# Matrix product with batch normalization: the last pair of tile 4 and the last chunk of tile 5 go back into the common order

## The chip, the cores and the metric

The kernel runs on one core of a Trainium2 chip. The metric is the device time of one execution in microseconds, as a median of several runs. Beside it stands one profiled execution, whose span is the time from its first to its last recorded instruction.

## The reference

The input `x` has 16 x 512 rows of 1024 numbers (8192 rows in all), the weight is 1024 x 768. Each of the 768 output columns is normalized over all 8192 rows and then scaled and shifted:

```python
y = np.matmul(x, weight)
mean = np.mean(y, axis=(0, 1), keepdims=True)
var = np.var(y, axis=(0, 1), keepdims=True)
y_norm = (y - mean) / np.sqrt(var + eps)
return (gamma * y_norm + beta).astype(np.float32)
```

No column can be written before its product is there for all 8192 rows, since its mean and variance need all of them.

## The kernel before

The 8192 rows are cut into C = 16 chunks of 512, the 768 columns into NT = 6 tiles of 128. Rows of `x` are loaded by GpSimd's queue as bf16 and transposed by VectorE into `xT`, one buffer for a chunk, so that TensorE can contract over K = 1024 in eight matmuls of 128.

Tiles 0 to 2 (GA = 3) are finished first, while `x` still arrives; their output follows while TensorE works on the rest. Tiles 3 to 5 are computed with the columns on the partitions: `mm` (L190) makes `y_ps`, 128 columns x 512 rows in one PSUM bank, by eight matmuls (L194). Chunks 0 to 4 of these tiles are done during the load, chunks 5 to 15 afterwards, tile by tile (loop at L559).

For each chunk of a tile, `bn` (L301) has VectorE take the statistics of the bank (`bn_stats`, six numbers, into `stats`), and `keep` (L332) has ScalarE copy the bank as bf16 into `y_sb`. After the 16th chunk the statistics are aggregated (`bn_aggr`), and mean and variance become a scale and a shift for each column: `finish_var` and `finish_affine` (L338, L344) for tiles 3 and 4, `finish` (L351) for tile 5. Then, for each tile:

- `norm` (L365) scales and shifts `y_sb` in place, on VectorE or ScalarE;
- `turn_y` (L377) puts 128x128 transposes on a list. `mm` takes one from this list behind each of its matmuls (`turn_one`, L386), so that the transposes run among the matmuls of the tile that follows;
- `out_copy` (L390) issues what is left of the transposes of its group and copies the PSUM bank `o_ps` to SBUF as f32 on ScalarE. For tiles 3 and 4 a group is a pair of chunks (128x1024) and goes into a piece of `ring`, a buffer of 6144 words in which pieces follow one another around; for tile 5 a group is one chunk (128x512) and goes into an `xT` buffer, called `o_sb`;
- `store` (L405) issues the DMA to HBM on SyncE's queue: 512 KB for a pair, 256 KB for a chunk, in runs of 512 bytes.

The order on every engine is written out by hand. Each step is put in a list with a time, `at(t, step, ...)`, in planned microseconds; the list is sorted by time, and `seq` (L75) ties each instruction to the one before it on its engine. `pe` is the planned time of TensorE. So the times only decide the order; the chip runs it as fast as data and buffers allow. Eight PSUM banks and the buffers of `ring` and `xT` go around in that order too.

At the end of the kernel two things leave the common way:

- HELD = 1: of the eight pairs of tile 4, `outputs` (L527) leaves out the last one (chunks 14 and 15). `held_outputs` (L539) puts its norms three planned microseconds before the end of tile 5's matmuls, and its transposes, copy and store right behind that end.
- The last chunk of tile 5 is done in two halves of 256 rows, in a bank each: `mm_half`, `bn_half`, `keep_half` (L315, L326, L329). The statistics of the first 14 chunks are aggregated beforehand by `sum_up` (L308) into one entry of `fin`; chunk 14 and the two halves add an entry each, and the aggregate in `finish` is over `fin`, 21 numbers for each column, in place of `stats`, 96 numbers.

`last_outputs` (L548) then does the 16 chunks of tile 5: all norms on VectorE, all copies on ScalarE.

Of the kernel before, what the change touches and what calls it, by code (L numbers as in the profile page):

```python
# [10 lines left out]
def kernel(  # L11
# [23 lines left out]
    nc = tc.nc  # L35
    f32 = mybir.dt.float32
    bf16 = mybir.dt.bfloat16
    AF = mybir.ActivationFunctionType
    ALU = mybir.AluOpType
# [5 lines left out]
    P = 128  # L45
    NT = N // P
    KQ = K // 4
    CH = 512
    RT = CH // P
    C = M // CH  # L50
    QR = 256
    QPC = CH // QR
    JW = KQ // 64
# [4 lines left out]
    GA = 3  # L58
    COLS = (0, 5, 10, 15)
    NA = GA * P  # L60
    HELD = 1
    GY = 3

    x_flat = x.flatten_outer_dims()
# [2 lines left out]
    singles = ctx.enter_context(tc.tile_pool(name="singles", bufs=1))  # L67
# [3 lines left out]
    psum = ctx.enter_context(tc.tile_pool(name="psum", bufs=8, space=bass.MemoryType.PSUM))  # L71
# [3 lines left out]
    def seq(bi):  # L75

        ins = bi.ins
        prev = last.get(ins.engine)
        if prev is not None:
            tc.add_manual_dep(  # L80
                ins, prev,
                mybir.DependencyInfo(mybir.DependencyClass.NoSync, mybir.DependencyReason.DATA),
                reason="order",
            )
        last[ins.engine] = ins.name
        return bi
# [10 lines left out]
    w_sb = singles.tile([P, JW, 2, N], bf16)  # L97
# [13 lines left out]
    stats = singles.tile([P, NT, C, 6], f32)  # L111
    ngamma = singles.tile([P, NT], f32)
    nscale = singles.tile([P, 1], f32)
    fin = singles.tile([P, 21], f32)
    msq = singles.tile([P, GA], f32)
    mv = singles.tile([P, NT, 2], f32)
    std = singles.tile([P, NT], f32)
# [7 lines left out]
    xs, xT, py, ygrp, yrow, ops, ost, aff = {}, {}, {}, {}, {}, {}, {}, {}  # L125
# [168 lines left out]
    def y(nt, c):  # L294
        key, i = ((nt, c // GY), c % GY) if nt >= GA else ((0, c), nt)
        if key not in ygrp:
            y_sb = ypool.tile([P, GY, CH], bf16, tag="y")
            ygrp[key] = y_sb
        return ygrp[key][:, i]

    def bn(nt, c):  # L301
        if (nt, c) == (NT - 1, C - 2):
            seq(nc.vector.bn_stats(fin[:, 3:9], py[nt, c]))
            return
        i = c if nt >= GA else COLS.index(c)
        seq(nc.vector.bn_stats(stats[:, nt, i, :], py[nt, c]))  # L306

    def sum_up():  # L308

        seq(nc.vector.memset(fin[:, 0:1], float((C - 2) * CH)))  # L310
        seq(nc.vector.bn_aggr(fin[:, 1:3], stats[:, NT - 1, 0:C - 2, :]))
        seq(nc.vector.tensor_scalar(
            fin[:, 2:3], fin[:, 2:3], float((C - 2) * CH), None, op0=ALU.mult))

    def mm_half(q):  # L315
        y_ps = psum.tile([P, CH], f32, tag="b")
        py["half", q] = y_ps[:, 0:QR]
        for jw in range(JW):
            for e in range(2):
                seq(nc.tensor.matmul(  # L320
                    y_ps[:, 0:QR], w_sb[:, jw, e, (NT - 1) * P:NT * P],
                    xT[C - 1][:, jw, q * QR:(q + 1) * QR, e],
                    start=(jw == 0 and e == 0), stop=(jw == JW - 1 and e == 1),
                ))

    def bn_half(q):  # L326
        seq(nc.vector.bn_stats(fin[:, 9 + 6 * q:15 + 6 * q], py["half", q]))

    def keep_half(q):  # L329
        seq(nc.scalar.copy(y(NT - 1, C - 1)[:, q * QR:(q + 1) * QR], py.pop(("half", q))))  # L330

    def keep(nt, c):  # L332
        seq(nc.scalar.copy(y(nt, c), py.pop((nt, c))))  # L333
# [16 lines left out]

    def finish(nt):  # L351
        one = slice(nt, nt + 1)
        src = stats[:, nt, :, :] if nt < NT - 1 else fin
        seq(nc.vector.bn_aggr(mv[:, nt, :], src))
        seq(nc.scalar.activation(std[:, one], mv[:, nt, 1:2], AF.Sqrt, bias=eps_sb, scale=1.0))
        seq(nc.vector.scalar_tensor_tensor(
            tmp[:, one], mv[:, nt, 0:1], -1.0, gamma_sb[:, one], op0=ALU.mult, op1=ALU.mult,
        ))
        seq(nc.vector.reciprocal(rstd, std[:, one]))
        seq(nc.vector.tensor_mul(scale[:, one], rstd, gamma_sb[:, one]))  # L360
        seq(nc.vector.scalar_tensor_tensor(
            shift[:, one], tmp[:, one], rstd, beta_sb[:, one], op0=ALU.mult, op1=ALU.add,
        ))
# [51 lines left out]
    def at(t, fn, *args):  # L415
        events.append((t, len(events), fn, args))
# [31 lines left out]
    pe = 0.0  # L448
# [12 lines left out]
    def unit(nt, c, span, jws=range(JW)):  # L461
        nonlocal pe
        pe = max(pe, arrive[c * RT + RT - 1])
        at(pe, mm, nt, c, jws)
        pe += span
        if jws[-1] == JW - 1:
            at(pe + 0.2, bn, nt, c)
            at(pe + 1.0, keep, nt, c)
# [13 lines left out]
    pe = max(pe, arrive["w", 2])  # L482
# [44 lines left out]
    def outputs(nt, t0, step):  # L527
        for b in range(C // 2):
            tb = t0 + step * b
            if nt == NT - 2 and b >= C // 2 - HELD:  # L530
                held.append(b)
                continue
            for i in range(2):
                at(tb - 2.2 + 0.5 * i, norm, nt, 2 * b + i, "act" if tb < tr + 2.0 and i == 0 else "dve")
            at(tb, turn_y, (nt,), 2 * b * CH, 2 * RT)
            at(tb + 2.2, out_copy, (nt,), 2 * b * CH, "act")
            at(tb + 2.3, store, (nt,), 2 * b * CH, 2 * RT)

    def held_outputs(nt, t0):  # L539

        for i, b in enumerate(held):
            for j in range(2):
                at(t0 - 3.0 + 0.4 * (2 * i + j), norm, nt, 2 * b + j, "dve")
            at(t0 + 0.05, turn_y, (nt,), 2 * b * CH, 2 * RT)
            at(t0 + 0.7 + 0.1 * i, out_copy, (nt,), 2 * b * CH, "act")
            at(t0 + 0.75 + 0.1 * i, store, (nt,), 2 * b * CH, 2 * RT)

    def last_outputs(nt, t0):  # L548

        for c in range(C):  # L550
            tb = t0 + 0.6 * c
            at(tb - 1.2, norm, nt, c, "dve")
            at(tb, turn_y, (nt,), c * CH, RT)
            at(tb + 0.5, out_copy, (nt,), c * CH, "act", True)
            at(tb + 0.6, store, (nt,), c * CH, RT)

    held = []
    halves = [range(JW // 2), range(JW // 2, JW)]
    for nt in range(GA, NT):  # L559
        for c in range(EARLY, C):  # L560
            if (nt, c) == (NT - 1, C - 1):
                for q in range(QPC):
                    at(pe, mm_half, q)
                    pe += 0.9
                    at(pe + 0.2, bn_half, q)
                    at(pe + (0.4 if q == 0 else 1.0), keep_half, q)
                at(pe - 2.4, sum_up)
                continue
            for jws in halves:
                unit(nt, c, MM_US / 2 + (0.12 if nt == GA else 0.17), jws)  # L570
        if nt < NT - 1:
            at(pe + 0.55, finish_var, nt)
            at(pe + 1.6, finish_affine, nt)
        else:
            at(pe + 0.55, finish, nt)
        if nt == GA:
            outputs(nt, S + 41.0, 2.0)
        elif nt < NT - 1:
            outputs(nt, pe + 4.6, 1.85)
        else:  # L580
            held_outputs(nt - 1, pe)
            last_outputs(nt, pe + 3.0)

    events.sort(key=lambda e: e[:2])
# [37 lines left out]
```

## Time and profile before

| what | us |
|---|---|
| median of 3 runs | 220.02 |
| lowest, highest run | 219.51, 225.25 |
| the profiled execution's own time | 220.02 |
| its span | 218.2 |
| PE busy (share of the span) | 199.1 (91%) |
| VectorE (DVE) busy | 151.5 (69%) |
| GpSimd (POOL) busy | 134.4 (62%) |
| ScalarE (ACT) busy | 120.4 (55%) |
| bytes read from HBM, written | 36.71 MB, 25.17 MB |

The span is 1.8 us shorter than the execution's time; what lies around it is not on the page. PE is TensorE's matmul side, PEld its weight loads, SP is SyncE, and a q behind an engine's name (SPq) marks its issuing of DMAs. L194 is line 194 of the kernel above. Times in a timeline are microseconds from the start of the span; "x7" counts instructions; what stands in brackets is the idle time ahead of an instruction and what ended it. A matmul's record is longer than its share of TensorE, since matmuls are pipelined; the chain of waits gives each one the time by which it moves the next.

The planned order by the time in the profile: the loads and tiles 0 to 2 take up to about 126 us; tile 3's matmuls, tile 4's and tile 5's follow, with the output of tiles 0 to 2, 3 and 4 running beside them; the last matmul of tile 5 ends at 197.6, its first store is issued at 200.8 and its last at 213.4.

### The profile page before, as it was taken

Reading aid. Unit: us, or ns where it says so; the run is one execution under the profiler, and the core shown is the slowest. Engines: PE = TensorE matmul, PEld = TensorE weight load, DVE = VectorE, ACT = ScalarE, POOL = GpSimd, SP = SyncE. Lnnn points to the kernel's source line nnn. Section 1 sums busy time; section 2 is a strip of 40 time slices with the busy share of each in tenths; the row PEclk is TensorE's granted clock in tenths of the full one; section 3 lists DMA queues with packets and bytes.
Section 4 is the critical chain, followed back from the end, with each engine's and each line's share of the span. In section 5 each row is a group of like instructions: output and inputs, shape, how many; then the busy total and the mean of one; then the engine's idle time right before and its main releaser. Section 6 shows DMA issues by size and latency. Waiting matters only on the chain.

```text
span 218.2 us, 3442 instructions
## 1 busy us (share of the span) xinstructions
PE 199.1 (91%) x1162; PEld 105.2 (48%) x1178; DVE 151.5 (69%) x264; ACT 120.4 (55%) x226; POOL 134.4 (62%) x153
## 2 busy tenths in 40 slices
PE   7997999999999999999999999999999999996500
PEld 2462454545554566545566544444444556555300
DVE  3221968886988889998744459988899999358400
ACT  2000562644453466645666414867766899977910
POOL 8787777778685599962658403999999960000000
PEclk9999999999999999999999999999999999999965
DMA  5999999999999999994000000698789799999997
GB/s 64 161 180 178 192 196 195 197 196 196 196 190 194 197 196 196 196 196 67 0 5 0 0 0 0 241 376 312 286 300 366 256 343 342 347 347 323 306 288 199
DMA packets 70161, 43.75 MB, mean 200 GB/s; under 512 B 4096, under 2 KB 69632, under 8 KB 70144
## 3 DMA queue, kind: packets, MB, share of 16 engines
q0 software_dynamic: 34624, 18.36, 61.7%
q1 hardware_dynamic: 35520, 25.18, 36.1%
q8 instruction: 9, 0.15, 0.3%
q14 instruction: 8, 0.07, 0.1%
HBM read 36.71 MB, written 25.17 MB: 284 GB/s over the span
## 4 chain that ended last, share of the span: by engine, by line
PE 74%; DVE 6%; DMA 5%; ACT 4%; POOL 3%; issue 3%; DVEq 0%; POOLq 0%
PE y_ps L194 40%; PE y_ps L184 29%; ACT o_sb L401 3%; PE o_ps L388 3%; DMA w_sb<-in_weight_dram 3%; DVE y_sb L372 3%; DMA ring<-in_x_dram 3%; POOL w_sb L147 2%; DVE ring L278 1%; DVE stats L306 1%; POOL ring L160 1%; PE y_ps L320 1%; PE a_ps L270 1%; PE tot_ps L230 1%; ACT ring L401 0%
## 5 line engine op out<-in xcount | busy, mean ns | idle before, releaser
L194 PE MATMUL y_ps<-xT_sb,w_sb 128*128 128x512 bf16 (+1 forms) x469 | 115.3, 382 | 2.8 <-DMA w_sb<-in_weight_dram 1.5
L194 PEld LDWEIGHTS <-w_sb 128*128 128x128 bf16 x484 | 46.1, 96 | 60.6 <-issue 3.4
L333 ACT CAST y_sb<-y_ps 128x512 bf16<-128x512 f32 x59 | 34.7, 589 | 52.3 <-DVE stats L306 49.5
L184 PE MATMUL y_ps<-w_sb,xT_sb 128*128 128x384 bf16 x384 | 63.4, 326 | 0.0
L306 DVE BATCH_NORM_STATS2 stats<-y_ps 128x6 f32<-128x512 f32 x58 | 39.2, 685 | 21.7 <-PE y_ps L194 21.4
L160 POOL DMA_DIRECT2D ring<-in_x_dram x72 | 45.3, 635 | 12.6 <-DVE xT_sb L172 6.5
L284 POOL TENSOR_TENSOR ring<-ring,sum 128x768 f32<-128x768 f32 x24 | 43.6, 1854 | 12.1 <-ACT sum L272 12.1
L184 PEld LDWEIGHTS <-xT_sb 128*128 128x128 bf16 x384 | 37.6, 98 | 25.6
L210 POOL TENSOR_TENSOR sum<-sum,sq_sb 128x384 f32<-128x384 f32 x38 | 38.2, 1006 | 18.2 <-ACT sq_sb L206 16.9
L172 DVE STREAM_TRANSPOSE xT_sb<-ring 128x1024 f32<-128x1024 f32 (+1 forms) x34 | 39.5, 1168 | 13.7 <-DMA ring<-in_x_dram 13.7
L388 PE MATMUL o_ps<-ident,y_sb 128*128 128x128 bf16 x240 | 36.2, 219 | 1.9 <-DVE y_sb L372 1.7
L213 DVE TENSOR_TENSOR sum<-y_ps,sum 128x384 f32<-128x384 f32 x48 | 26.1, 544 | 14.2 <-ACT sq_sb L206 13.2
L206 ACT ACTIVATE sq_sb<-y_ps 128x384 f32<-128x384 f32 x48 | 23.4, 492 | 15.0 <-PE y_ps L184 11.8
L219 ACT CAST y_sb<-y_ps 128x384 bf16<-128x384 f32 x48 | 22.8, 476 | 7.6 <-DVE sum L213 7.3
L401 ACT CAST ring<-o_ps 128x1024 f32<-128x1024 bf16 (+1 forms) x24 | 22.3, 951 | 5.3 <-PE o_ps L388 3.1
L278 DVE TENSOR_TENSOR ring<-y_sb,a_ps 128x768 f32<-128x768 bf16 x24 | 22.4, 939 | 0.0
L388 PEld LDWEIGHTS <-y_sb 128*128 128x128 bf16 x240 | 19.0, 97 | 4.9 <-DVE y_sb L372 1.8
L372 DVE TENSOR_SCALAR y_sb<-y_sb,scale,shift 128x512 bf16<-128x512 bf16 x44 | 17.5, 457 | 0.0
L367 ACT ACTIVATE y_sb<-y_sb,shift,scale 128x512 bf16<-128x512 bf16 x16 | 12.6, 812 | 0.0
L153 PE MATMUL idle_ps<-idle_sb 128*128 128x512 bf16 x37 | 11.2, 472 | 1.2 <-DVE idle_sb L101 1.2
L401 ACT CAST o_sb<-o_ps 128x512 f32<-128x512 bf16 x16 | 8.0, 662 | 0.3 <-PE o_ps L388 0.3
L153 PEld LDWEIGHTS <-idle_sb 128*128 128x128 bf16 x38 | 4.3, 115 | 7.5 <-issue 3.9
(60 smaller groups left out, 39.4 us busy)
## 6 DMA issues: line engine op xcount, KB each, us to landing
ring<-in_x_dram POOLq DMA_DIRECT2D x56, 256.0 KB, 8.8
out_dram<-ring SPq DMA_DIRECT2D x32, 384.0 KB, 3.3
out_dram<-ring SPq DMA_DIRECT2D x16, 512.0 KB, 5.9
out_dram<-o_sb SPq DMA_DIRECT2D x16, 256.0 KB, 3.7
ring<-in_x_dram POOLq DMA_DIRECT2D x16, 128.0 KB, 5.5
w_sb<-in_weight_dram POOLq DMA_DIRECT2D x8, 96.0 KB, 4.9
w_sb<-in_weight_dram POOLq DMA_DIRECT2D x4, 192.0 KB, 5.8
gamma_sb<-in_gamma_dram SPq DMA_DIRECT2D x6, 0.5 KB, 4.7
```

The costliest lines, as they stand in the source:

```text
L160: seq(nc.gpsimd.dma_start(x_bf[32 * i:32 * i + 32], src[:, :, KQ * i:KQ * (i + 1)]))
L172: seq(nc.vector.transpose(dst[:, half, :, jw0:jw1], src[:, :, jw0:jw1]))
L184: seq(nc.tensor.matmul(y_ps, xT[c][:, jw, s * P:(s + 1) * P, e], w_sb[:, jw, e, 0:NA], start=(jw == 0 and e == 0), stop=(jw == JW - 1 and ...
L194: seq(nc.tensor.matmul(y_ps, w_sb[:, jw, e, nt * P:(nt + 1) * P], xT[c][:, jw, q0 * QR:q1 * QR, e], start=(jw == 0 and e == 0 and q0 == 0) ...
L210: seq(eng.tensor_add(acc, acc, py.pop(("sq", c, s))))
L213: seq(nc.vector.tensor_add(sum1, py["row", c, s][:, 0:NA], sum1))
L278: seq(nc.vector.tensor_mul(o_sb, yrow[c][:, s:s + 2], aff[0][:, None, :].to_broadcast([P, 2, NA]),))
L284: seq(nc.gpsimd.tensor_add(o_sb, o_sb, sum1[:, None, :].to_broadcast([P, 2, NA])))
L306: seq(nc.vector.bn_stats(stats[:, nt, i, :], py[nt, c]))
L333: seq(nc.scalar.copy(y(nt, c), py.pop((nt, c))))
L388: seq(nc.tensor.transpose(dst, src, ident))
L401: seq(nc.scalar.copy(o_sb, src))
```

## The change

The change takes both special ways at the end out again. The last pair of tile 4 is treated by `outputs` like the other seven: its norms, transposes, copy and store get planned times at the same step of 1.85 behind the pair before, which puts the eight transposes among the first four matmuls of chunk 14 of tile 5. The last chunk of tile 5 is one `unit` like the others: eight matmuls over 512 rows, one `bn_stats`, one `keep`. `sum_up`, `mm_half`, `bn_half`, `keep_half`, `held_outputs` and the tile `fin` are gone, and `finish` aggregates the 16 entries of `stats`. Nothing else is changed; the order of the stores on SyncE's queue stays the same. The diff, cut to its core:

```diff
-    HELD = 1
...
     def bn(nt, c):
-        if (nt, c) == (NT - 1, C - 2):
-            seq(nc.vector.bn_stats(fin[:, 3:9], py[nt, c]))
-            return
         i = c if nt >= GA else COLS.index(c)
         seq(nc.vector.bn_stats(stats[:, nt, i, :], py[nt, c]))
...
-    def sum_up():
-        seq(nc.vector.memset(fin[:, 0:1], float((C - 2) * CH)))
-        seq(nc.vector.bn_aggr(fin[:, 1:3], stats[:, NT - 1, 0:C - 2, :]))
-        seq(nc.vector.tensor_scalar(
-            fin[:, 2:3], fin[:, 2:3], float((C - 2) * CH), None, op0=ALU.mult))
-    def mm_half(q):
...
-    def bn_half(q):
...
-    def keep_half(q):
...
     def finish(nt):
         one = slice(nt, nt + 1)
-        src = stats[:, nt, :, :] if nt < NT - 1 else fin
-        seq(nc.vector.bn_aggr(mv[:, nt, :], src))
+        seq(nc.vector.bn_aggr(mv[:, nt, :], stats[:, nt, :, :]))
...
     def outputs(nt, t0, step):
         for b in range(C // 2):
             tb = t0 + step * b
-            if nt == NT - 2 and b >= C // 2 - HELD:
-                held.append(b)
-                continue
...
-    def held_outputs(nt, t0):
...
         for c in range(EARLY, C):
-            if (nt, c) == (NT - 1, C - 1):
-                for q in range(QPC):
-                    at(pe, mm_half, q)
-                    pe += 0.9
-                    at(pe + 0.2, bn_half, q)
-                    at(pe + (0.4 if q == 0 else 1.0), keep_half, q)
-                at(pe - 2.4, sum_up)
-                continue
             for jws in halves:
                 unit(nt, c, MM_US / 2 + (0.12 if nt == GA else 0.17), jws)
...
         else:
-            held_outputs(nt - 1, pe)
             last_outputs(nt, pe + 3.0)
```

More of the change, by code (lines that the diff above doesn't have):

```diff
@@ L113 @@
     nscale = singles.tile([P, 1], f32)
-    fin = singles.tile([P, 21], f32)
     msq = singles.tile([P, GA], f32)
@@ L301, in bn @@
     def bn(nt, c):
-        if (nt, c) == (NT - 1, C - 2):
-            seq(nc.vector.bn_stats(fin[:, 3:9], py[nt, c]))
-            return
         i = c if nt >= GA else COLS.index(c)
         seq(nc.vector.bn_stats(stats[:, nt, i, :], py[nt, c]))
-    def sum_up():
-        seq(nc.vector.memset(fin[:, 0:1], float((C - 2) * CH)))
-        seq(nc.vector.bn_aggr(fin[:, 1:3], stats[:, NT - 1, 0:C - 2, :]))
-        seq(nc.vector.tensor_scalar(
-            fin[:, 2:3], fin[:, 2:3], float((C - 2) * CH), None, op0=ALU.mult))
-    def mm_half(q):
[L316 to L324, printed above, removed]
-    def bn_half(q):
-        seq(nc.vector.bn_stats(fin[:, 9 + 6 * q:15 + 6 * q], py["half", q]))
-    def keep_half(q):
-        seq(nc.scalar.copy(y(NT - 1, C - 1)[:, q * QR:(q + 1) * QR], py.pop(("half", q))))
     def keep(nt, c):
@@ L537, in outputs @@
             at(tb + 2.3, store, (nt,), 2 * b * CH, 2 * RT)
-    def held_outputs(nt, t0):
[L541 to L546, printed above, removed]
     def last_outputs(nt, t0):
@@ L555, in last_outputs @@
             at(tb + 0.6, store, (nt,), c * CH, RT)
-    held = []
     halves = [range(JW // 2), range(JW // 2, JW)]
```

## The prediction

> **What bounds the kernel now.** I read the page first, then the busy time of each engine in stretches of the last 40 us, then the order of time around the last statistics, then SyncE's issues. The chain of waits is 74% TensorE, and the diff touches only the part after the matmuls of tile 4, so only the end of that chain matters. What limits the end is told by the stretches (columns: stretch, length, busy time of PE, PEld, DVE, ACT, POOL, granted clock, DMA share, GB/s):
>
> ```profile
> 195.00:200.00 5.00, 3.34 (x31) 2.43 (x30) 3.99 (x15) 2.99 (x7) 0.00 (x0) 1.00 1.15 345
> 200.00:205.00 5.00, 4.96 (x62) 3.38 (x60) 4.51 (x14) 4.85 (x11) 0.00 (x0) 1.00 1.03 302
> 205.00:210.00 5.00, 0.00 (x0) 0.00 (x0) 0.00 (x0) 3.15 (x7) 0.00 (x0) 0.85 1.04 293
> 210.00:214.00 4.00, 0.00 (x0) 0.00 (x0) 0.00 (x0) 0.00 (x0) 0.00 (x0) 0.50 1.03 285
> ```
>
> The DMA engines move 345 GB/s while TensorE still multiplies, and go on at 285 to 300 GB/s for 9 us after TensorE is done. The end is a stream of stores; other engines matter only where they leave this stream without work. A finer cut shows that this happens once:
>
> ```profile
> 200.00:200.25 0.25, 0.25 (x6) 0.21 (x4) 0.25 (x2) 0.10 (x1) 0.00 (x0) 1.00 0.82 240
> 200.25:200.50 0.25, 0.25 (x7) 0.15 (x5) 0.25 (x2) 0.25 (x1) 0.00 (x0) 1.00 0.15 43
> 200.50:200.75 0.25, 0.25 (x5) 0.15 (x4) 0.25 (x2) 0.25 (x2) 0.00 (x0) 1.00 0.88 270
> ```
>
> Against 348 GB/s the three quarters lack 0.08, 0.22 and 0.06 us: a hole of 0.36 us. SyncE's issues say whose it is:
>
> ```profile
> 187.16 10.51 SPq L406 DMA_DIRECT2D out_dram<-ring  x7
> 199.62 0.37 SPq L406 DMA_DIRECT2D out_dram<-ring  x1
> 200.76 0.37 SPq L406 DMA_DIRECT2D out_dram<-o_sb  x1
> 212.51 1.75 SPq L406 DMA_DIRECT2D out_dram<-o_sb  x2
> ```
>
> Seven 512 KB stores go out back to back, 1.50 us each, which is 349 GB/s: the queue holds SyncE back, so it has a backlog. The last 512 KB store, that of the held pair, comes 1.95 us after the seventh is through (197.67); by then the backlog is running out, and the hole is the wait for it. Its data begin at about 200.57, so 0.95 us pass from issue to data. From there the stream doesn't stop: 512 KB at 348 GB/s take 1.50 us, and sixteen o_sb stores follow. What makes the held store late is the chain of the last statistics:
>
> ```profile
> 195.63 1.98 PE L320 MATMUL y_ps<-xT_sb,w_sb 128*128 128x256 bf16 x16
> 197.45 0.61 PE L388 MATMUL o_ps<-ident,y_sb 128*128 128x128 bf16 x8
> 197.64 0.43 DVE L327 BATCH_NORM_STATS2 fin<-y_ps 128x6 f32<-128x256 f32 x1 [0.48 <-PE y_ps L320]
> 198.11 0.25 DVE L354 BATCH_NORM_AGGREGATE mv<-fin 128x2 f32<-128x21 f32 x1
> 198.60 0.99 ACT L401 CAST ring<-o_ps 128x1024 f32<-128x1024 bf16 x1
> 199.72 0.72 PE L388 MATMUL o_ps<-ident,y_sb 128*128 128x128 bf16 x8 [1.66 <-DVE y_sb L372]
> 200.15 0.59 ACT L401 CAST o_sb<-o_ps 128x512 f32<-128x512 bf16 x1 [0.28 <-PE o_ps L388]
> ```
>
> The held pair's eight transposes and its copy lie in the shadow of this chain. The chain ends in the first o_sb copy, and that in the store issued at 200.76.
>
> **The change part by part.** The sum is made against the profiled execution, 218.2 us of span in a time of 220.02 us, which is also the median of the three runs.
>
> *The held pair goes back among the matmuls.* In the built order its eight transposes stand between the first matmuls of chunk 14 of tile 5. TensorE is full there, and the chain of waits has the price:
>
> ```profile
> 193.36 0.06 PE o_ps L388
> 193.42 0.22 PE y_ps L194
> 193.64 0.06 PE o_ps L388
> 193.70 0.23 PE y_ps L194
> 193.92 0.06 PE o_ps L388
> 193.98 0.91 PE y_ps L194 x4
> ```
>
> A matmul with a transpose takes 0.28 us, one without 0.91/4 = 0.228: 0.055 a transpose, eight make 0.44 us, all of it ahead of the last statistics. Lower end 0 (TensorE waits there anyhow; the stretch is fully busy, so this is far), upper end 0.61, the row where the eight stood alone.
>
> *The last chunk in one piece.* Eight 512-column matmuls at 0.228 are 1.82 us; the sixteen halves took 1.83 on the chain of waits: nothing. But the last statistics are over 512 columns instead of 256, and the last aggregate over 96 numbers instead of 21:
>
> ```profile
> L306 DVE BATCH_NORM_STATS2 stats<-y_ps 128x6 f32<-128x512 f32 x58 | 39.2, 685 | 21.7 <-PE y_ps L194 21.4 <-remote 0.3
> L340 DVE BATCH_NORM_AGGREGATE mv<-stats 128x2 f32<-128x96 f32 x2 | 1.2, 582 | 0.0
> ```
>
> That is 0.685 - 0.432 = 0.25 us and 0.582 - 0.249 = 0.33 us, both on the chain. Removed are a memset, an aggregate (0.53) and a multiply (0.15) on VectorE; they ran at 195.2 to 195.9, beside TensorE, and held chunk 14's statistics back by 0.07 us at most, which the last chunk doesn't see. They give nothing.
>
> *What moves on the other engines.* VectorE: two norms (0.41 each) come earlier, where it idles 1.55 us ahead of each statistics instruction. ScalarE: the held copy (1.0 us) now stands behind the copy of the eleventh pair and ahead of the evictions of chunks 13 and 14. The transposes end at 193.98 + 4 x 0.228 + 0.44 = 195.33, so copy and evictions (1.0 + 0.59 + 0.59) are done at about 197.6 (chunk 14's statistics end near 197.0), and the square root behind them is due at 199.4: 1.8 us of cover. Its ring piece is the sixth back, whose store was issued at 188.65 and with the median 6.0 us landed at 194.6, before 195.33. The eviction of chunk 15, now 0.59 behind the square root instead of 0.99 + 0.38, ends at 200.3; the first o_sb copy is due at 201.2. SyncE: no store changes its place; the held store finds its data at 196.4 and queues behind the eleventh, which leaves at 197.67.
>
> *The sum.* The chain slips by 0.44 + 0.25 + 0.33 = 1.02 us (0.58 to 1.19 by the ends). The first o_sb store is issued at 200.76 + 1.02 = 201.78, its data start 0.95 later, at 202.73. The held store's data now follow without a hole: where the stream ran dry at about 200.2 they go on, and 1.50 us later, at about 201.7, it runs dry again. Before, the o_sb data could start at 200.57 + 1.50 = 202.07. So the stream of sixteen starts 202.73 - 202.07 = 0.66 us later and ends as much later: the old hole of 0.4 is closed, a new one of 1.0 opens behind it. 220.02 + 0.66 = 220.7 us. By the ends of the slip the term is 0.22 to 0.83, and 220.2 to 220.9.
>
> The Trainium skill, "DMA: Bandwidth & Descriptors", section "Latency and other measured facts", puts the first byte of a SyncE-issued transfer at some 0.6 us; by it alone the o_sb data would start at 202.38 and the time be 220.3. The 0.95 us from 199.62 to the refilled stream is this kernel's own row, and I keep it.
>
> **The rivals.**
>
> *The hole doesn't count.* In the quarter of the hole 43 GB/s still flow, two of sixteen engines' worth (348/16 = 21.8 each): some engines lag. If the laggards set when the last store lands, they work through old and new hole, and the end stays: 220.0 us. For it speaks the unbroken 1.50 us beat of the 512 KB stores; against it that the last 13 us move 285 to 300 GB/s, so the laggards have caught up long before the end. If instead the slip itself were covered, the closed hole would give 219.6; that takes a first o_sb store issued before 200.7, a slip below zero, and no row gives one.
>
> *The moved copy blocks ScalarE: slower.* The copy of the held pair stands ahead of the square root. Were its ring piece not free, everything behind it would wait. It decides once the copy starts after 199.4 - 0.59 - 0.59 - 1.0 = 197.2. If it had to wait for the eleventh store (196.28 + 6.0 = 202.3), the end would slip by 5 more: 225.8 us. Against it: such waits on a store's landing cost ScalarE 0.5 us once in the last 38 us, and the sixth store back has landed 2.6 us before that point.
>
> *TensorE's clock falls.* TensorE waits 1.66 us before the last transposes now, and then from 198.05 (197.61 + 0.44) to 200.74 (199.72 + 1.02), 2.7 us. The granted clock reaches 0.50 only at 208.5, 3.5 us after its last work at 205.0. If it fell at 2.7, the four transposes of the first chunk would take 0.23 longer; behind it the copies (0.48 a chunk) hide the rest. 220.9 us.
>
> **How the numbers follow.** Forecast as summed 0.72; the hole doesn't count (or is gained) 0.14; clock 0.08; ScalarE blocked 0.03; 0.03 for what I don't see. The time is the likeliest's, 220.7. The range takes in 219.6 with a little of the scatter of the undisturbed runs (0.51 between 219.51 and 220.02) below, and the clock case with the upper end of the slip, 220.9 + 0.17, and twice that scatter above: 219.4 to 222.0. Two per cent, about what a measurement of this kernel can tell from no change, are 4.4 us; only the blocked ScalarE and part of the unseen reach that: slower 0.05, same 0.93, faster 0.02.
>
> **What would show it.** Right: the last matmul of chunk 15 ends at about 198.05, the aggregate takes 0.58 us, the held store is issued at 197.8 right behind the eleventh, the first o_sb store at 201.8; the DMA rate has no dip at 200.3 but one of about 1 us before 202.7; the last two issues end near 214.9. Wrong: a last matmul at 197.6 (the transposes were free); no dip, or an unchanged end in spite of the dip (the laggards decide); a square root that waits for ScalarE's queue; transposes of the last tile at half the granted clock.

## The result, and the profile after

| what | before | after |
|---|---|---|
| median, us | 219.84 (6 runs) | 225.91 (6 runs) |
| lowest, highest | 219.51, 225.25 | 225.01, 226.85 |
| ratio of after to before, 95% interval | | 1.0278 (1.0247 to 1.0308) |
| profiled execution: time, span | 220.02, 218.2 | 225.01, 223.2 |

The change made the kernel 2.8% slower in this comparison; 220.7 us were forecast, and no measurable change. One run of the kernel before took as long as the runs after, 225.25 us, and the ratio leaves it out; it stood in the table from the start, and it will matter.

**Where the 5 us are.** Of the two profiled executions the stretches are laid side by side, before first, then after (columns: stretch, length, busy time of PE, PEld, DVE, ACT, POOL, granted clock, DMA share, GB/s):

```profile
170.00:175.00 5.00, 5.00 (x38) 2.68 (x36) 4.64 (x10) 4.09 (x8) 5.00 (x4) 1.00 0.90 307
175.00:180.00 5.00, 4.94 (x42) 2.91 (x41) 5.00 (x9) 5.00 (x11) 3.21 (x2) 1.00 1.04 339
180.00:185.00 5.00, 4.93 (x43) 2.94 (x42) 5.00 (x14) 5.00 (x8) 0.00 (x0) 1.00 1.06 342
```

```profile
170.00:175.00 5.00, 4.39 (x31) 2.02 (x27) 5.00 (x7) 3.63 (x6) 3.65 (x2) 1.00 0.66 225
175.00:180.00 5.00, 3.65 (x23) 1.74 (x24) 4.64 (x7) 1.47 (x4) 2.98 (x2) 1.00 0.89 295
180.00:185.00 5.00, 3.52 (x30) 2.08 (x31) 5.00 (x9) 5.00 (x10) 2.59 (x2) 1.00 0.39 123
```

TensorE was full between 170 and 185 us; after, it stands still for 3.4 us of these 15 (0.61 + 1.35 + 1.48), and the stores run at 123 GB/s at the end of them. All of this lies ahead of the first instruction that the change adds, moves or removes. The orders part first on VectorE, behind its statistics of 189.46 in before (193.64 in after), where the pair's two norms now stand; until then both kernels issue the same instructions in the same order on every engine. At 166 us the two VectorE timelines part (columns: start, duration, engine, line, operation, out<-in; L372 before is L342 after). Before:

```profile
166.29 1.02 DVE L372 TENSOR_SCALAR y_sb<-y_sb,scale,shift 128x512 bf16<-128x512 bf16 x1
167.23 0.94 DVE L278 TENSOR_TENSOR ring<-y_sb,a_ps 128x768 f32<-128x768 bf16 x1
...
168.70 0.45 DVE L372 TENSOR_SCALAR y_sb<-y_sb,scale,shift 128x512 bf16<-128x512 bf16 x1
169.07 0.94 DVE L278 TENSOR_TENSOR ring<-y_sb,a_ps 128x768 f32<-128x768 bf16 x1
...
170.54 0.46 DVE L372 TENSOR_SCALAR y_sb<-y_sb,scale,shift 128x512 bf16<-128x512 bf16 x1
```

After:

```profile
166.31 2.83 DVE L342 TENSOR_SCALAR y_sb<-y_sb,scale,shift 128x512 bf16<-128x512 bf16 x1
169.07 0.94 DVE L276 TENSOR_TENSOR ring<-y_sb,a_ps 128x768 f32<-128x768 bf16 x1
...
170.54 1.53 DVE L342 TENSOR_SCALAR y_sb<-y_sb,scale,shift 128x512 bf16<-128x512 bf16 x1
171.99 0.94 DVE L276 TENSOR_TENSOR ring<-y_sb,a_ps 128x768 f32<-128x768 bf16 x1
...
173.46 1.52 DVE L342 TENSOR_SCALAR y_sb<-y_sb,scale,shift 128x512 bf16<-128x512 bf16 x1
```

The instruction is a norm of tile 3, in place in SBUF, in a stretch where GpSimd adds the shift rows of tiles 0 to 2 to `ring` (`shift_rows`, about 1.8 us an addition). It is asked for at the same moment, 166.3 us, with one addition under way that began at 165.32 and the next due at 167.11. Before, the norm went in at the seam between the two. After, it waited through the second as well. What follows is the GpSimd timeline of after (in brackets: idle time ahead, and what ended it):

```profile
165.32 3.67 POOL L282 TENSOR_TENSOR ring<-ring,sum 128x768 f32<-128x768 f32 x2
170.09 1.83 POOL L282 TENSOR_TENSOR ring<-ring,sum 128x768 f32<-128x768 f32 x1 [1.09 <-DVE ring L276]
173.01 1.83 POOL L282 TENSOR_TENSOR ring<-ring,sum 128x768 f32<-128x768 f32 x1 [1.09 <-DVE ring L276]
```

Before, eleven additions ran there without a gap:

```profile
158.15 20.06 POOL L284 TENSOR_TENSOR ring<-ring,sum 128x768 f32<-128x768 f32 x11
```

After, VectorE is late with the product (L276) that GpSimd needs; each addition starts the moment the product is done, and so always ahead of the next norm, which waits until it ends. The two engines go in step, 2.92 us for a pair of row blocks in place of 1.85. The product of L276 is 1.84 us late the first time, then 2.92, 3.98 and 5.05: 1.81 for the first norm and three times 1.07. TensorE waits for norms through the transposes behind them: twice 0.50 us for VectorE's, and 2.23 us for one of ScalarE's. That one stands, in ScalarE's order, behind a square root that waited 3.53 us for the aggregate of tile 4, which VectorE reached late:

```profile
179.30 0.29 ACT L312 ACTIVATE std<-mv,eps_sb 128x1 f32<-128x1 f32 x1 [3.53 <-DVE mv L311]
181.48 0.23 PE L358 MATMUL o_ps<-ident,y_sb 128*128 128x128 bf16 x1 [2.23 <-ACT y_sb L337]
```

The eleventh 512 KB store (the last but one of them, just ahead of the held pair's) is issued at 201.21 instead of 196.28, 4.93 us later; the first `o_sb` store 5.21 later, the last issue 5.05 later (218.47 for 213.42). Counted along TensorE, whose last matmul ends 4.61 us later (202.21 for 197.61), 0.44 of the 5.05 are the transposes of the moved pair (shown below), 4.17 the norms' wait, and the other 0.45 lie behind the last matmul.

**The end itself** went as the prediction said, in shape. The stretches and the order of time of after:

```profile
206.50:206.75 0.25, 0.25 (x7) 0.21 (x4) 0.25 (x2) 0.25 (x1) 0.00 (x0) 1.00 1.02 303
206.75:207.00 0.25, 0.25 (x7) 0.15 (x5) 0.25 (x2) 0.25 (x2) 0.00 (x0) 1.00 0.49 150
207.00:207.25 0.25, 0.25 (x5) 0.15 (x4) 0.25 (x2) 0.25 (x1) 0.00 (x0) 1.00 0.99 295
```

```profile
199.34 2.88 PE L192 MATMUL y_ps<-xT_sb,w_sb 128*128 128x512 bf16 x12
199.66 1.01 ACT L371 CAST ring<-o_ps 128x1024 f32<-128x1024 bf16 x1 [0.41 <-DMA out_dram<-ring]
202.25 0.70 DVE L301 BATCH_NORM_STATS2 stats<-y_ps 128x6 f32<-128x512 f32 x1 [1.11 <-PE y_ps L192]
202.98 0.59 DVE L324 BATCH_NORM_AGGREGATE mv<-stats 128x2 f32<-128x96 f32 x1
204.93 1.36 PE L358 MATMUL o_ps<-ident,y_sb 128*128 128x128 bf16 x16 [2.71 <-DVE y_sb L342]
205.97 0.37 SPq L376 DMA_DIRECT2D out_dram<-o_sb  x1
```

The held pair's store follows the eleventh at once (202.70 behind 201.21), the old dip in the DMA rate is gone, and a new one stands ahead of the `o_sb` data. The first norm comes 2.24 us after the last matmul, before 1.64: +0.60 for a forecast of 0.58 (0.25 + 0.33). The new hole is 0.03 + 0.14 + 0.04 = 0.21 us against 348 GB/s, where 1.0 was forecast.

### The profile page after: what moved, and what is told of

Same layout as the page of the kernel before. It is cut to its first block, busy times and chain, and to the rows that moved or that the text cites. A ratio compares the mean times of both kernels' runs of the same rounds, so it can differ in the third digit from the quotient of the medians.

```text
span 223.2 us, 3421 instructions
## 1 busy us (share of the span) xinstructions
PE 199.1 (89%) x1154; PEld 103.9 (47%) x1170; DVE 156.2 (70%) x260; ACT 119.0 (53%) x225; POOL 134.2 (60%) x153
## 4 chain that ended last, share of the span: by engine, by line
PE 73%; DVE 8%; DMA 5%; ACT 4%; issue 3%; POOL 3%; DVEq 0%; ACTq 0%; POOLq 0%
PE y_ps L192 40%; PE y_ps L182 28%; DVE y_sb L342 3%; PE o_ps L358 3%; ACT o_sb L371 3%; DMA w_sb<-in_weight_dram 3%; DMA ring<-in_x_dram 2%; DVE ring L276 2%; DVE stats L301 2%; POOL w_sb L145 2%; POOL ring L158 1%; PE a_ps L268 1%; PE tot_ps L228 1%; ACT y_sb L337 0%; ACT y_sb L304 0%
## 5 line engine op out<-in xcount | busy, mean ns | idle before, releaser
L192 PE MATMUL y_ps<-xT_sb,w_sb 128*128 128x512 bf16 (+1 forms) x477 | 117.8, 382 | 3.5 <-DMA w_sb<-in_weight_dram 2.4
L192 PEld LDWEIGHTS <-w_sb 128*128 128x128 bf16 x492 | 46.9, 96 | 61.6 <-issue 4.3
L304 ACT CAST y_sb<-y_ps 128x512 bf16<-128x512 f32 x60 | 35.3, 588 | 54.0 <-DVE stats L301 52.1
L301 DVE BATCH_NORM_STATS2 stats<-y_ps 128x6 f32<-128x512 f32 x60 | 40.5, 685 | 21.3 <-PE y_ps L192 20.7
L358 PE MATMUL o_ps<-ident,y_sb 128*128 128x128 bf16 x240 | 36.7, 219 | 6.3 <-DVE y_sb L342 3.7
L342 DVE TENSOR_SCALAR y_sb<-y_sb,scale,shift 128x512 bf16<-128x512 bf16 x44 | 22.5, 569 | 0.0
L276 DVE TENSOR_TENSOR ring<-y_sb,a_ps 128x768 f32<-128x768 bf16 x24 | 22.4, 940 | 0.0
L151 PE MATMUL idle_ps<-idle_sb 128*128 128x512 bf16 x37 | 10.4, 445 | 1.2 <-DVE idle_sb L100 1.2
```

The source lines that it names most:

```text
L192: seq(nc.tensor.matmul(y_ps, w_sb[:, jw, e, nt * P:(nt + 1) * P], xT[c][:, jw, q0 * QR:q1 * QR, e], start=(jw == 0 and e == 0 and q0 == 0) ...
L276: seq(nc.vector.tensor_mul(o_sb, yrow[c][:, s:s + 2], aff[0][:, None, :].to_broadcast([P, 2, NA]),))
L342: seq((nc.vector if eng == "dve" else nc.gpsimd).tensor_scalar(y(nt, c), y(nt, c), scale[:, nt:nt + 1], shift[:, nt:nt + 1], op0=ALU.mult, ...
L358: seq(nc.tensor.transpose(dst, src, ident))
```

## The experiments

The first question was whether the change causes the lost 5 us. Theory A said yes, by where buffers lie: without `fin`, 84 bytes a partition, the tiles behind it move (`xT` by 96 bytes). The rivals: any kernel may lose here, by chance or by the chip.

**The buffer put back.** After, with `fin`'s place filled:

```diff
     nscale = singles.tile([P, 1], f32)
+    pad = singles.tile([P, 21], f32)
```

> The changed kernel with an unused tile of 21 numbers where the tile fin stood, so that every buffer behind it has its old SBUF address (xT from 62112 on instead of 62016); no instruction differs from the changed kernel. Theory A (VectorE's norms of tile 3 and GpSimd's shift additions compete for one SBUF port pair, and the 96-byte shift of the buffers decides who gets it at 167 us): the norm at 166.3 takes about 1.0 us again, the 5 us stall is gone, and only the end of the kernel differs: 220.0 to 220.9 us. Theory B (the same competition, but decided by something else, such as where instructions lie or chance): stays at 225 to 226 us. Theory C (the reordered end itself costs the 6 us): stays at 225 to 226 us, with the stall behind 195 us.

Measured: 225.84 us (10 runs, 224.77 to 227.16), the first norm 2.81 us. Theory A falls: with the old addresses the norm still loses. More: the kernel before, run beside it on the same chip, now took 224.67 us itself (25 runs, 222.57 to 226.84). Ratio 1.0037 (0.9998 to 1.0075).

**Other places.** After and before, each with a pad of 32 bytes a partition (`[P, 8]`):

> The changed kernel with an unused tile of 32 bytes in that place: the buffers start at 62048, an odd multiple of 32 like before the change, but not at the old addresses. Theory A with the alignment to 64 bytes as what counts: 220.0 to 220.9 us. Theory A with the exact address, or theory B: either of 220.5 and 225.9, and no reason for one of them. Theory C: 225 to 226 us.

> The kernel before with 32 bytes more in that place: the buffers start at 62144, a multiple of 64 as after the change. Theory A with the alignment to 64 bytes: the norm of tile 3 at 166.3 loses, a stall of about 5 us, 224.5 to 225.5 us. Theory A with the exact address, or theory B: 219.8 or 225, no reason for one. Theory C: 219.8 us, nothing at the end is changed.

Measured: 224.87 us, ratio 1.0019 (0.9988 to 1.0051), first norm 2.83; and 225.19 us, ratio 1.0004 (0.9965 to 1.0044), first norm 2.78. The profile of the second is the kernel before with the loss in it. Place alone doesn't decide.

**Fewer additions.** The last 8 of the 24 additions are left out, so that none runs beside the norms:

```diff
+    group = 0
...
-                at(tr + 1.1, shift_rows, c, s)
+                if group < 16:
+                    at(tr + 1.1, shift_rows, c, s)
+                group += 1
```

> The changed kernel with the last 8 of 24 shift additions on GpSimd left out (rows of tiles 0 to 2 in those groups lack their shift). Theories A and B: nobody competes for the port any more, the four norms of tile 3 take 0.41 us each instead of 2.83, 1.53, 1.52, 1.53, TensorE doesn't wait at 170 to 185 us, and the time is 219.5 to 220.9 us. Theory C: stays at 225 to 226 us, since the end is not touched.

> The kernel before with the last 8 of 24 shift additions on GpSimd left out (rows of tiles 0 to 2 in those groups lack their shift). Theory B: nobody competes, so the stall is gone wherever it was: 219.3 to 220.3 us on any chip, 4 to 5 us below the kernel before where that one loses, about its time where that one wins; and 0.5 to 1.0 us below the 221.0 us of the changed kernel with the same omission. Theory C (the end costs the 6 us): as the kernel before on the same chip.

Measured: after 220.99 us (5 runs, 219.94 to 223.28; ratio to the kernel before on its chip 0.9791, 0.9742 to 0.9841), before 219.67 us (0.9775, 0.9742 to 0.9808). VectorE in the second, whose next three norms took 0.40 as well:

```profile
165.11 0.40 DVE L372 TENSOR_SCALAR y_sb<-y_sb,scale,shift 128x512 bf16<-128x512 bf16 x1
```

With no addition beside it a norm takes 0.40 us, and the 5 us are gone from both kernels. So the loss needs the additions beside the norms. But some work is left out with them, and nothing waits for GpSimd's pace any more; that it is the norms' wait is shown below, by norms that don't compete.

**After once more**, beside the kernel before on one chip:

> The changed kernel again, beside the kernel before on the same chip. Theory A is fallen: the buffers' old addresses left the stall in place, and on that chip the kernel before itself took 224.7 us. Theory B now reads: both kernels can lose or win the port at the first norm of tile 3 (worth 5 us), and what the change itself is worth is the slower end, 0.5 to 1.0 us. Then where both lose or both win, the difference is 0.5 to 1.0 us (ratio 1.002 to 1.005), and where only the changed one loses it is 6 us again. Theory D (the changed kernel loses more often than the one before for a reason in it): on a chip where the kernel before wins, the changed one still loses, 225 to 226 us against 219.8.

Measured: 225.27 us (12 runs) beside 224.61 (17 runs), ratio 1.0011 (0.9975 to 1.0048). Where both lose, the two kernels can't be told apart by this.

**Norms that don't compete.** All work is kept. The seven norms beside the additions become `scalar_tensor_tensor`, with the shift read from a spare column of the PSUM bank `a_ps`:

```diff
+            aff["tail"] = a_ps[:, NA:NA + 1]
...
+            seq(nc.scalar.copy(aff["tail"], shift[:, one]))
...
+            seq(nc.vector.scalar_tensor_tensor(
+                y(nt, c), y(nt, c), scale[:, nt:nt + 1], aff["tail"].to_broadcast([P, CH]),
+                op0=ALU.mult, op1=ALU.add,
+            ))
```

> The changed kernel, all of its work done, with the seven VectorE norms of tile 3 that stand beside GpSimd's additions taken as y * scale + shift with the shift read from a spare PSUM column as a tensor, one input in SBUF and one in PSUM. Theory B: such an instruction doesn't compete with GpSimd; it takes about 0.6 us whatever GpSimd does, the products follow without a stall, and the time is 220.3 to 221.3 us on any chip. If it is the waiting for something else than the port, the norms stay at 1.5 to 2.8 us and the time at 225.

> The kernel before with the same seven norms. Theory B: 219.7 to 220.6 us on any chip, 0.5 to 1.0 us below the changed kernel with the same norms, 4 to 5 us below the kernel before where that one loses the port. If the port isn't the cause: as the kernel before on the same chip, or slower by up to 1 us.

Measured: after 220.46 us, ratio 0.9812 (0.9778 to 0.9845); before 219.38 us, ratio 0.9769 (0.9736 to 0.9802). The group of the norms and GpSimd's additions, in before with this edit:

```profile
L371 DVE SCALAR_TENSOR_TENSOR y_sb<-y_sb,scale,a_ps 128x512 bf16<-128x512 bf16 x7 | 5.0, 732 | 0.0
```

```profile
162.51 12.67 POOL L286 TENSOR_TENSOR ring<-ring,sum 128x768 f32<-128x768 f32 x7
```

Each takes 0.73 us whatever GpSimd does, and GpSimd runs these seven without a gap: 12.67/7 = 1.81 an addition. So the loss is the norms' wait for GpSimd. This version is faster than both kernels wherever they lose; its 219.4 against the 219.84 where the kernel before doesn't come from different sessions, and show no difference. It also shows what the change costs by itself, so its two parts were tried on it, on one chip.

**The parts of the change**, on the norms that don't compete: none (before), the held pair put back alone (`HELD = 0`), the last chunk whole alone, and both (after).

> The kernel before with the seven norms of tile 3 in the form that doesn't use the shared port, again, as the base for the three beside it. 219.0 to 219.8 us on any chip, by the 219.38 it took before.

> The base with the held pair back among the matmuls, the last chunk still in halves: the first part of the change alone. By the prediction's terms the chain slips by 0.44 us for the eight transposes and the held store's hole of about 0.4 us is closed, but a new one of about the slip opens: 0.0 to 0.3 us over the base, with the last matmul 0.44 us later against its stores. Rival: TensorE has slack there and it gains 0.2 to 0.4 us.

> The base with the last chunk in one piece and the pair still held: the second part alone. The chain gets longer by 0.25 + 0.33 = 0.58 us, and the held store, which waits on ScalarE behind the square root, comes 0.58 us later too: 0.5 to 0.7 us over the base. Rival: the stores' backlog hides it, 0.0 to 0.2 us over.

> The changed kernel with the same norms, again: both parts of the change without the port. The prediction's sum is 0.66 us over the base; the run before measured 1.08. Theory B expects 0.5 to 1.3 us over the base.

| kernel | median, us | lowest, highest | ratio to the kernel before |
|---|---|---|---|
| none | 219.24 | 218.70, 219.60 | 0.9764 (0.9734 to 0.9794) |
| held pair back | 219.54 | 219.09, 222.37 | 0.9795 (0.9747 to 0.9844) |
| last chunk whole | 220.22 | 219.22, 221.22 | 0.9811 (0.9773 to 0.9850) |
| both | 220.58 | 219.07, 221.23 | 0.9819 (0.9782 to 0.9857) |

Six runs each; the intervals overlap, and the 0.3 of the held pair is not above the scatter. Over the 12 runs of none (219.37 on average) and the 12 of both (220.48), on this chip (those of the preceding experiment among them), the change costs 1.1 us, with an interval of 0.45 each way from their scatter (standard deviations 0.42 and 0.62). The stretches of both show the new hole, and the clock in it:

```profile
201.00:201.25 0.25, 0.25 (x5) 0.25 (x4) 0.25 (x2) 0.25 (x1) 0.00 (x0) 0.50 0.92 271
201.25:201.50 0.25, 0.25 (x5) 0.25 (x3) 0.25 (x2) 0.25 (x2) 0.00 (x0) 0.50 0.16 47
201.50:201.75 0.25, 0.25 (x6) 0.25 (x4) 0.25 (x2) 0.25 (x1) 0.00 (x0) 0.50 0.14 43
201.75:202.00 0.25, 0.25 (x5) 0.25 (x4) 0.25 (x2) 0.25 (x2) 0.00 (x0) 0.50 0.39 119
```

By the same sum as in the prediction this is 0.06 + 0.22 + 0.22 + 0.16 = 0.65 us. And the stretches of none where the old hole should be:

```profile
198.50:199.50 1.00, 0.81 (x11) 0.62 (x12) 1.00 (x4) 0.71 (x3) 0.00 (x0) 1.00 1.15 348
199.50:200.50 1.00, 1.00 (x15) 0.71 (x14) 1.00 (x5) 1.00 (x3) 0.00 (x0) 0.95 1.15 347
200.50:201.50 1.00, 1.00 (x13) 0.97 (x10) 1.00 (x5) 1.00 (x3) 0.00 (x0) 0.50 1.15 345
```

There is none: the stores run through.

**Does the moment decide who goes in?** Theory E: how far ahead of the next addition the norm asks. On the kernel before, 1, 4, 8 or 12 dead memsets (0.10 us each, 0.16 apart) on GpSimd, behind its first addition, shift that distance. Theory F: it doesn't decide.

```diff
+    dead = singles.tile([P, 1], f32)
...
+        if (c, s) == (1, 0):
+            for _ in range(4):
+                seq(nc.gpsimd.memset(dead, 0.0))
```

> The kernel before with one dead one-column memset on GpSimd behind its first shift addition, so that the 23 that follow come some 0.1 us later against VectorE. Theory E (where in GpSimd's running addition VectorE's norm asks for the port decides: asked 0.83 us ahead of the next addition it won, at 0.79 to 0.81 it lost): at about 0.9 us it wins, first norm 1.1 us long, 219.8 to 220.6 us. Theory F (chip or state decides, not the moment): loses as the kernel before does on this chip, 224.5 to 225.5 us, first norm 2.9 us long.

> The same with four memsets, some 0.4 us later: the norm asks about 1.2 us ahead of the next addition. Theory E: the outcome differs between some of these four kernels on one chip, 220 us where it wins and 225 where it loses. Theory F: all four as the kernel before.

> The same with eight memsets, some 0.8 us: the norm asks about 1.6 us ahead of the next addition. If it loses, the first norm takes about 1.6 + 1.8 = 3.5 us and the time is 225.5; if it wins, 1.8 us and 220.5. Theories E and F as for the four memsets.

> The same with twelve memsets, some 1.2 us: the norm asks about 0.2 us ahead of the next addition. In the won case of the kernel before, norms that asked 0.26 to 0.28 us ahead all won and took 0.45 us. Theory E: it wins, 219.5 to 220.5 us. Theory F: loses, first norm about 2.2 us, 224.5 us.

| memsets | median, us | runs | ratio to the kernel before (224.80) | asked ahead of the next addition, us | first norm, us |
|---|---|---|---|---|---|
| 1 | 224.52 | 10 | 0.9987 (0.9946 to 1.0027) | 0.85 | 2.83 |
| 4 | 225.07 | 10 | 1.0021 (0.9987 to 1.0054) | 1.45 | 3.43 |
| 8 | 225.72 | 10 | none, see below | 0.27 | 4.04 |
| 12 | 227.15 | 4 | 1.0117 (1.0054 to 1.0180) | 0.89 | 4.64 |

The distances are not those expected, since each memset took 0.16 us of GpSimd's time and not 0.10; the short one came with 8. With 8 and 12 the first norm lets two further additions pass, as VectorE and GpSimd of the kernel with 8 show:

```profile
165.19 4.04 DVE L376 TENSOR_SCALAR y_sb<-y_sb,scale,shift 128x512 bf16<-128x512 bf16 x1
```

```profile
163.66 5.42 POOL L285 TENSOR_TENSOR ring<-ring,sum 128x768 f32<-128x768 f32 x3
170.17 1.83 POOL L285 TENSOR_TENSOR ring<-ring,sum 128x768 f32<-128x768 f32 x1 [1.09 <-DVE ring L279]
```

It asks at 165.19; additions that begin at about 165.5 and 167.3 go ahead of it, and it comes in when GpSimd has none ready. Theory E falls: all four distances lose, 0.27 us too, with which a later norm of the kernel before had won. Of the ten runs with 8 memsets one took 219.05 us, the others 223.85 to 226.93: by its size it won, and a ratio of such a mixture says nothing. So one kernel on one chip can go either way.

## Why the prediction was wrong

1. **The step that failed: "only the end of that chain matters".** The sum added the end's difference to 220.02 us, as if the 196 us ahead of it were fixed because no instruction in them moves. They were not: from the first of tile 3's norms to the last matmul the kernel after takes 35.9 to 37.3 us in four profiles where that norm loses its place beside GpSimd, and 31.75 in three where it can't; the order is the same. That the norms' wait is the cause was shown by leaving the additions out (both kernels near 220 us) and by norms that don't compete (the same, with all work done).
2. **Whose loss it is.** The 2.8% are not the cost of the change where the two were compared again: there the kernel before loses as well (224.6 to 224.8 us on three chips) and the ratio is 1.0011 (0.9975 to 1.0048). In the first comparison before lost once in six runs, judged by its 225.25 us alone, since it was not profiled, and after six times in six. Whether the change tipped it there, or the chip of those runs, or chance, stays open: no later chip let the kernel before win, so the pair was not compared there again. Buffer places and the moment of asking were tried and don't decide.
3. **The signs that I passed over.** The run of 225.25 us stood in the table of before, and the range was built on "the undisturbed runs (0.51 between 219.51 and 220.02)", without asking what that run was. And the profile of before named the place. Its group of norms, and a stretch of its VectorE timeline:

```profile
L372 DVE TENSOR_SCALAR y_sb<-y_sb,scale,shift 128x512 bf16<-128x512 bf16 x44 | 17.5, 457 | 0.0
```

```profile
176.10 2.58 DVE L372 TENSOR_SCALAR y_sb<-y_sb,scale,shift 128x512 bf16<-128x512 bf16 x3
```

The mean is 457 ns where one alone takes 400; three that should take 1.2 us at most took 2.58, beside an addition. The same group in after has 5.0 us more, so the comparison of the two pages points at the place:

```profile
L342 DVE TENSOR_SCALAR y_sb<-y_sb,scale,shift 128x512 bf16<-128x512 bf16 x44 | 22.5, 569 | 0.0
```

"SBUF — State Buffer", section "Who interferes with whom" (the Trainium skill), says that VectorE's instructions of this form and GpSimd take turns at one pair of ports, whole instructions at a time, and that a form with at most one SBUF input outside the two-port modes keeps out of it: 0.40, 1.53 and 2.83 us on one side, 0.73 always on the other, agree. It also says that whoever issues first gets the ports; here a norm that already waited was passed by one or two additions that began later, and the measurement decides.

4. **The slip of the chain: right.** Last matmul 0.44 later in both than in none (197.03 for 196.59), as forecast; the norm behind it +0.60 for 0.58.
5. **The hole: it moves as forecast, but it doesn't set the end.** The distance between the two issues that enclose a hole, less 3.0 to 3.3 us, gives it in five profiles:

| kernel | between the issues of | distance, us | hole in the stretches, us |
|---|---|---|---|
| before | eleventh and held store | 3.34 | 0.36 |
| none | eleventh and held store | 3.12 | 0.02 |
| after | held store and first `o_sb` | 3.27 | 0.21 |
| both | held store and first `o_sb` | 3.91 | 0.65 |
| both, preceding experiment | held store and first `o_sb` | 3.68 | 0.45 |

The prediction's own figures (197.8 and 201.78) are 3.98 apart, 0.7 to 1.0 by this. How large the hole comes out depends on how far the stores lag behind TensorE: the eleventh is issued 1.00 us ahead of the last matmul's end in after, 1.33 in before, and 2.00 in after with the place of `fin` filled, where almost nothing is stored for a whole microsecond:

```profile
206.00:207.00 1.00, 1.00 (x15) 0.71 (x14) 1.00 (x4) 1.00 (x3) 0.00 (x0) 1.00 0.19 55
```

But the end doesn't follow the hole. It follows the last matmul, in all eighteen profiles (us; "held up" means that the norms of tile 3 lost their place):

| end of the kernel | profiles | first norm of tile 3 to last matmul's end | last matmul's end to last issue |
|---|---|---|---|
| as before, norms not held up | before; fewer additions; norms that don't compete, twice | 31.32 | 15.81 to 15.85 |
| as before, norms held up | 32-byte pad; 1, 4, 8, 12 memsets | 36.6 to 38.8 | 15.83 to 15.89 |
| held pair back alone | norms that don't compete | 31.75 | 15.85 |
| last chunk whole alone | norms that don't compete | 31.31 | 16.41 |
| as after, norms not held up | fewer additions; norms that don't compete, twice | 31.75 | 16.24, 16.24, 16.46 |
| as after, norms held up | after, twice; two pads | 35.9 to 37.3 | 16.23 to 16.28 |

So the sum's credit of 0.36 for the old hole (0.66 in place of 1.02) was the mis-sized term: before and none have holes of 0.36 and 0.02 and the same end. What the change gives back is 0.16 to 0.20 us in three pairs of profiles: from the first `o_sb` issue to the last pass 12.50 us in after and 12.66 in before, where the held pair's store goes out right ahead of them. With 0.43 for the transposes and 0.60 for the chain that makes 0.83 to 0.87 us in place of 0.66, within the measured 1.1 and its interval; both adds 0.22 for its clock. In the preceding experiment's pair of profiles, 1.15 us more stand at the first norm of tile 3 already (166.46 for 165.31), ahead of everything that the change touches; what makes them is open, and so is what sets the 12.5 us of the sixteen stores.

6. **The rivals.** That the hole doesn't count came true, by the table above, but the unchanged end that this rival drew from it did not: the slip counts, less 0.16 to 0.20. ScalarE's moved copy did wait for a store to land, 0.41 us (the row at 199.66), and nothing came of it; that this rival was priced at 225.8 us, close to the measured 225.91, is a coincidence: nothing behind that copy was late by it. TensorE's clock fell in the wait in some executions and not in others: in both it was 0.52 at 199 to 200 us, the first `o_sb` store came 1.72 us behind the norm instead of 1.51, and that 0.2 is what the rival had priced at 0.23; in after, and in the preceding experiment's profile of the same kernel as both, the same wait of 2.7 us kept it at 1.00. "TensorE: Matmul & The Clock Gate", Part 1 (the Trainium skill), has a free-running window of some 3.4 us, which would let equal waits end differently; no run here shows the window itself.

## What to carry to other kernels

A sum over the changed part holds only if the unchanged part repeats: look at the outlier among the runs of before, and in the groups for an instruction whose mean stands well over its shortest time, and ask what it costs if that goes the other way. Where VectorE's in-place SBUF work runs beside back-to-back GpSimd work, one instruction that comes in late can put the two engines in step, and a form that reads its second operand from PSUM, slower alone (0.73 for 0.40 us), avoids it. A hole in a stream of stores need not move the end: here holes of 0.02 and 0.36 us had the same end, so ask first which instruction the last stores hang on, and count from there.

## What the hardware did that I had not expected

- A waiting VectorE instruction did not get the next turn: one (2.83 us) or two additions (4.04 and 4.64 us) that began after it asked went first. One seam won or lost sets the pace of the next three pairs, 1.85 or 2.92 us each.
- The kernel before has two times, about 219.8 and 224.7 us, by which of the two happens: five short and one long in the first comparison, and all 78 runs between 222.57 and 227.48 us on the three chips of the later ones. The kernel with 8 memsets showed both on one chip (219.05 us once in ten).
- From the last matmul's end to the last issue the kernel before took 15.81 to 15.89 us in nine profiles, whether the stores had stood still for 0.02 us or for 0.36 ahead of it.
- The granted clock went to 0.50 in none at 200.5 us, while transposes ran (PE busy 1.00 of 1.00 in that stretch).
